# Moving the late rows' normalization from the first two feed-forward groups to the third to sixth, and giving the last output-projection blocks all PSUM banks

## The chip, the cores and the metric

The kernel runs on one core of a Trainium2 chip. The metric is the device time of one execution in microseconds; before the change its median over three runs is 2681.76 us (2677.7 to 2685.48).

The core's engines have instruction queues of their own and run them in order: PE (matmuls, with its weight loads shown apart as PEld), DVE (vector), ACT (scalar and activation), POOL (general elementwise) and SP, which here only issues DMA transfers. Semaphores tie the queues together.

## The reference

One layer of a transformer-like block over 2048 rows of width 1024, in float32: a normed input projection, two kinds of attention, an output projection onto the residual, and a gated feed-forward network of width 2816.

```python
u = rms_norm(h, norm1_w[l])
proj = jnp.einsum('bsd,de->bse', u, w_in[l])
...
mix = jnp.concatenate([y_diff.reshape(b, s, DIFF_HEADS * DIFF_V_DIM),
                       y_sb.reshape(b, s, SB_HEADS * SB_DIM)], axis=-1)
h = h + jnp.einsum('bse,ed->bsd', mix, w_out[l])

u2 = rms_norm(h, norm2_w[l])
gate = jnp.einsum('bsd,df->bsf', u2, w_gate[l])
up = jnp.einsum('bsd,df->bsf', u2, w_up[l])
h = h + jnp.einsum('bsf,fd->bsd', jax.nn.silu(gate) * up, w_down[l])
```

Here `y_diff` is a differential attention (two softmax maps per head) and `y_sb` a stick-breaking attention.

## The kernel before

**Number format.** Every float32 operand is scaled and split into two float16 parts, high and low, and a product is three matmuls (high by high, high by low, low by high). Splitting an operand takes a pass for the high part and one on DVE for the low part (`split_weight`, L221 is the low part).

**Stages.** The 2048 rows are 16 blocks of 128. First come projections and attention, then the output projection (`out_proj`, L832 the matmuls, tiles `po`; L835 the evictions from PSUM onto the residual, on DVE), one call of `next(op)` per block. Its result goes to DRAM as `hd`. The blocks 0 to 11 are normed, transposed (`xtr`) and split at once (`post`), and stored as `xcd`, the left operand of the feed-forward network. The blocks 12 to 15, the **late rows**, are only stored in `hd`; they are needed in the second half of the feed-forward work alone.

**Feed-forward.** The rows are taken in two halves of 1024. Each half runs over 11 groups of 256 columns of the 2816 (`steps`, index `i`, 0 to 21). A group has a `gate` and an `up` product, each as seven block products of a Strassen-like scheme (`quad`, 12 matmuls of 512 columns each: tiles `pa`, `pm`, `pd`), with DVE combining and evicting them (L1047, L1052, L1057, L1067, L1071), and every second group has the `down` product of two groups between its gate and its up (groups 2, 4, 6, 8, 10). In the first half the weights are prepared as they go: `load_ffn` fetches a float32 stage (`stages`, two buffers in turn), squares it on ACT (`sq`, L954, L190), sums the columns with PE (`fsc`, L963 or L183), makes a power-of-two scale and splits (L216 to L221), and stores the result in DRAM (`split`), from which the second half reads it.

**The late rows before.** `build_x` is a generator for the two pairs of blocks (`j` = 2, 3). A tick runs it to its next `yield`: load two row blocks (`bx<-hd`), norm them (L226 on ACT, L229 on DVE), transpose on PE (L1213) and copy back on ACT, then form and split the seven blocks that the scheme needs (`x_ops`) and store them to `xcd`. One tick comes ahead of the first down weight, the others at fourteen places of the groups 0 and 1 (`late_at`). It takes the four `hs` buffers (which `down` uses for the residual rows from group 2 on) and one of the two `wd` buffers. The stage of the second up weight is issued behind the late rows' first two loads (`rows`).

**What sets the order.** The Tile layer schedules the program: it takes the instructions with their dependencies and orders each engine's queue by its own timeline. `high_priority` (PRI) and `issue_after` bend it. So a small edit moves instructions on all engines. PSUM has eight banks: in the feed-forward part `pst` hands them out in turn, six of pool `ps2` and two of pool `psj`; the output projection uses the two of `psj`. `hs`, `act` (the activations, two buffers) and `cg`, `cu` are SBUF tiles with a fixed number of buffers.

Of the kernel before, what the change touches and what calls it, by code (L numbers as in the profile page):

```python
# [11 lines left out]
F32 = mybir.dt.float32  # L12
F16 = mybir.dt.float16
# [3 lines left out]
ALU = mybir.AluOpType  # L17
# [42 lines left out]
def block(tc, a, out):  # L60
# [3 lines left out]
    with top:  # L64
# [192 lines left out]
        with ExitStack() as ph1:  # L257
# [557 lines left out]
            def out_proj():  # L815
                for t in range(NT):
                    mt = pp.tile([P, 2 * D], F16, tag="xt", bufs=3, name=nm("mt"))[:].rearrange("p (k n) -> p k n", k=KT)
                    with tc.high_priority(PRI["wm"]) if PRI["wm"] else nullcontext():
                        mts.append(SP.dma_start(mt, ms[t]))
                    if t in spare:  # L820
                        xf = spare[t].bitcast(F32)
                    else:
                        xf = pp.tile([P, 4, 4, 2, 64], F16, tag="st", name=nm("xf"))[:].rearrange("p c t s e -> p (c t s e)").bitcast(F32)
                    SP.dma_start(xf, x[t * P : (t + 1) * P, :])
                    for h in range(2):
                        po = psj.tile([P, 512], F32, tag="pj", name=nm("po"))
                        for n in range(2):
                            q = 0
                            sl = slice(256 * n, 256 * n + 256)
                            for kt in range(KT):  # L830
                                for xi, wi in ((0, 0), (0, 1), (1, 0)):
                                    PE.matmul(po[:, sl], lhsT=mt[:, kt, P * xi : P * xi + P], rhs=wos[2 * h + n][wi][:, kt, :], start=q == 0, stop=q == 23)  # L832
                                    q += 1
                            xl = xf[:, 512 * h + 256 * n : 512 * h + 256 * n + 256]
                            DVE.scalar_tensor_tensor(xl, po[:, sl], kos[2 * h + n][:], xl, op0=ALU.mult, op1=ALU.add)  # L835
                    note("D", 1400)
                    SP.dma_start(hd[t], xf)
                    if t >= 12:
                        yield
                        continue  # L840
                    post(t, xf)
                    yield
# [31 lines left out]
        with ExitStack() as ph2:  # L874
# [18 lines left out]
            r_2, p_2, r_24 = rp2  # L893
            scales = {}

            rows = []
            front = [None]

            def behind():
# [5 lines left out]
            def stage(fg, nme):  # L905
                st = stages[:, turn[0]]
                turn[0] ^= 1
                f0 = 256 * fg
                with tc.issue_after(rows[1].ins) if (fg, nme) == (1, "u") else nullcontext():
                    fetch(st, f0, nme)  # L910
                store(0)
                return st

# [161 lines left out]
            def gate(W, X, hooks):  # L1075
# [11 lines left out]
                note("A", 2000)  # L1087
                return sg

            def up(W, X, sg, hooks, final=False):  # L1090
                if final:
                    act = stages[:].rearrange("p b n -> p (b n)").bitcast(F16)[:, :7168].rearrange("p (o s n) -> p o s n", o=7, s=2)
                else:
                    act = fp.tile([P, 7, 2, 512], F16, tag="act", bufs=2, name=nm("act"))

                def put(o, src):
                    ACT.copy(act[:, o, 0], src)  # L1097
                    note("A", 500)
                    tt(act[:, o, 1], src, act[:, o, 0], ALU.subtract, 512, LE)

                def on_up(f, t, c):
                    s = sg[f, t][:]
                    DVE.scalar_tensor_tensor(s, c[:], W["F"][:], s, op0=ALU.mult, op1=ALU.mult)  # L1103
                    if (f, t) != (0, 1):
                        put({(0, 0): 0, (1, 0): 1, (1, 1): 3}[f, t], s)
                        return
                    a11, a12, a21, a22 = (sg[k][:] for k in ((0, 0), (1, 0), (0, 1), (1, 1)))
                    s3 = fp.tile([P, 512], F32, tag="cu", bufs=CU, name=nm("cu"))
                    tt(s3[:], a11, a21, ALU.subtract, 512, SE)
                    tt(a21, a21, a22, ALU.add, 512, SE)  # L1110
                    put(2, a21)
                    tt(a11, a21, a11, ALU.subtract, 512, SE)
                    tt(a12, a12, a11, ALU.subtract, 512, SE)
                    put(6, a12)
                    put(4, a11)
                    put(5, s3[:])

                quad(W["u"], X, "cu", CU, on_up, hooks)
                note("D", 2440)
                return act  # L1120
# [66 lines left out]
                        SP.dma_start(out[t * P : (t + 1) * P, :] if last else hd[t], hs[j][q][:])  # L1187

            def build_x():
                w2f, xa, xb, xt = (hp.tile([P, D], F32, tag="hs", bufs=4, name=nm("bx")) for _ in range(4))  # L1190
                SP.dma_start(w2f[:], a["norm2_w"].partition_broadcast(P))
                DVE.tensor_scalar(w2f[:], w2f[:], r_24[:], None, op0=ALU.mult)
                b16 = fd.tile([P, 7, 2, 512], F16, tag="wd", bufs=2, name=nm("b16"))[:].rearrange("p o s n -> p (o s n)")
                n = [0]

                def bufs():
                    n[0] = (n[0] + 1) % 3
                    return b16[:, 2048 * n[0] : 2048 * n[0] + 2048]

                d2 = lambda z: z[:].rearrange("p (d n) -> p d n", d=2)  # L1200
                for j in (2, 3):
                    for q, z in enumerate((xa, xb)):
                        rows.append(SP.dma_start(z[:], hd[8 + 2 * j + q]))
                    yield
                    for z in (xa, xb):
                        norm_tile(z[:], z[:], w2f[:], xt[:])
                    yield
                    for z in (xa, xb):
                        for h in range(2):
                            tr = pst("xtr")  # L1210
                            with behind():
                                for k in range(4):
                                    PE.transpose(tr[:, P * k : P * k + P], z[:, 512 * h + P * k : 512 * h + P * k + P], id32[:])  # L1213
                            ACT.copy(z[:, 512 * h : 512 * h + 512], tr[:])
                        note("A", 1000)
                    yield
                    yield from x_ops([d2(z) for z in (xa, xb)], d2(xt), 1, j, bufs, "AP", "DP")

            W = {}
            X = [None] * 7  # L1220
# [25 lines left out]
                for _ in range(n):  # L1246
                    next(ticks, None)

            tick(1)
            load_now(0, 0, "d", W)  # L1250

            steps = [(h, f) for h in range(2) for f in range(NFG)]
            units = []
            hs = None
            chains = {}
            late_at = ((5, 9, 10, 11, 12, 13, 14), (3, 7, 8, 9, 10, 11, 12))
            for i, (half, fg) in enumerate(steps):
                if i == NFG:
                    load_x(1, XL)
# [13 lines left out]
                    go(key)  # L1273

                def row(s):
                    if i < 2 and s in late_at[i]:
                        tick(1)

                def in_gate(s):
# [66 lines left out]
```

## Time and profile before

| what | value |
|---|---|
| median of three runs | 2681.76 us (2677.7 to 2685.48) |
| the profiled execution | 2682.59 us, of which the span from the first to the last instruction is 2680.8 |
| mean granted clock of PE | 0.984 of full speed |
| PE busy | 2492.4 us (93%) |
| DVE, POOL, ACT busy | 1932.7 (72%), 1489.1 (56%), 1347.0 us (50%) |
| output projection, from first to last matmul | 1179.9 to 1426.9 us |
| feed-forward, from its first to its last gate or up product | 1427.2 to 2621.4 us |
| packets of the main DMA queue | 69.9% of 16 engines' span |

A row of a timeline gives the start and duration in us, the engine, line and operation, the tiles written and read without their numbers, shapes, how many such instructions follow each other, and in brackets how long the engine was idle before it and what released it. L98 and L89 are helpers that many places use, so there the tile names tell the place. PE's matmuls are pipelined: a row's duration is a little longer than the distance to the next one.

### The profile page before, as it was taken

The numbers are of one execution on the slowest core, as the hardware profiler recorded it, in microseconds if no ns is written. First come the engines' busy times: TensorE is split into PE (matmuls) and PEld (weight loads), VectorE is DVE, ScalarE is ACT, GpSimd is POOL, SyncE is SP. The second block draws the span as 40 slices with busy tenths as digits, with TensorE's granted clock in tenths as the row PEclk, the third lists the DMA queues.
The fourth block names the chain that finished last, engine by engine and source line by source line (L and its number), as shares of the span: only waits on it lengthen the run. The fifth ranks groups of instructions, "written<-read, shape, count | busy, mean of one in ns | idle before, by whom it ended". The sixth has DMA issues, their size and how long they took to land. (4 is left out here: it accounts for less than half of the span.)

```text
span 2680.8 us, 50579 instructions
## 1 busy us (share of the span) xinstructions
PE 2492.4 (93%) x19628; PEld 1498.6 (56%) x19628; DVE 1932.7 (72%) x3711; ACT 1347.0 (50%) x2487; POOL 1489.1 (56%) x1098
## 2 busy tenths in 40 slices
PE   6998989888988989889989899999999999999999
PEld 4655656577776776557775344444444444444444
DVE  6898969898989989877766868777685544444434
ACT  4665656567978878665644535344352112111121
POOL 2578667667767766546764656565564232322323
PEclk9999999999999999999999899999999999999999
DMA  6777697767998979987897574665649743635532
GB/s 222 213 162 181 146 200 168 179 143 184 193 179 179 185 160 209 210 191 217 218 285 282 208 250 178 255 226 202 245 183 346 293 177 143 233 141 186 195 111 95
DMA packets 619585, 534.41 MB, mean 199 GB/s; under 512 B 480640, under 2 KB 548224, under 8 KB 609104
## 3 DMA queue, kind: packets, MB, share of 16 engines
q1 hardware_dynamic: 617520, 529.09, 69.9%
q8 instruction: 154, 2.52, 0.4%
q0 software_dynamic: 512, 1.36, 0.2%
q14 instruction: 87, 0.71, 0.1%
q10 hardware_dynamic: 1312, 0.72, 0.1%
HBM read 261.08 MB, written 147.32 MB: 152 GB/s over the span
## 5 line engine op out<-in xcount | busy, mean ns | idle before, releaser
L98 POOL TENSOR_TENSOR s<-z,s 128x1024 f16<-128x1024 f32 (+7 forms) x288 | 472.0, 1647 | 142.5 <-ACT s L89 109.8
L507 PE MATMUL sc<-kT,qT 128*128 128x512 f16 (+3 forms) x1520 | 382.0, 353 | 53.3 <-DVE z L623 19.3
L622 DVE TENSOR_TENSOR_SCAN z<-z,sc 128x512 f32<-128x512 f32 (+3 forms) x320 | 352.8, 1112 | 58.6 <-ACT sc L620 38.0
L1138 PE MATMUL pd<-wd,act 128*128 128x512 f16 x1764 | 390.9, 379 | 1.2 <-DVE cg L1071 1.2
L326 PE MATMUL pj<-w,xt 128*128 128x384 f16 x1920 | 352.2, 331 | 18.8 <-ACT xt L683 6.9
L1030 PEld LDWEIGHTS <-wg 128*128 128x128 f16 x1848 | 182.0, 99 | 230.2 <-issue 16.4
L518 PE MATMUL yp<-v,aT 128*128 128x64 f16 (+1 forms) x4896 | 269.8, 204 | 41.6 <-DMA aT<-s 40.2
L518 PEld LDWEIGHTS <-aT 128*128 128x128 f16 x4896 | 237.5, 99 | 120.4 <-DMA aT<-s 52.5
L1030 PEld LDWEIGHTS <-wu 128*128 128x128 f16 x1848 | 180.7, 98 | 218.0 <-issue 2.6
L98 POOL TENSOR_TENSOR act<-cg,act 128x512 f16<-128x512 f32 x112 | 148.5, 1337 | 262.9 <-ACT act L1097 150.8
L1138 PEld LDWEIGHTS <-act 128*128 128x128 f16 x1764 | 172.8, 98 | 209.4 <-issue 2.8
L326 PEld LDWEIGHTS <-xt 128*128 128x128 f16 x1920 | 187.3, 99 | 147.5 <-issue 21.4
L89 ACT CAST s<-z 128x128 f16<-128x128 f32 (+7 forms) x215 | 173.1, 809 | 134.1 <-DMA aT<-s 40.5
L98 POOL TENSOR_TENSOR hs<-hs,cu 128x512 f32<-128x512 f32 x99 | 130.9, 1328 | 171.3 <-DVE hs L1144 70.8
L619 ACT ACTIVATE z<-sc,c 128x512 f32<-128x512 f32 (+3 forms) x320 | 210.7, 663 | 25.6 <-PE sc L507 11.7
L1097 ACT CAST act<-cg 128x512 f16<-128x512 f32 x126 | 77.3, 616 | 238.4 <-DVE cg L1103 162.7
L507 PEld LDWEIGHTS <-qT 128*128 128x128 f16 x1520 | 128.4, 99 | 121.0 <-DVE z L623 23.0
L832 PE MATMUL po<-wo,mt 128*128 128x256 f16 x1536 | 180.7, 277 | 13.9 <-DVE xf L835 8.4
L1030 PE MATMUL pm<-X,wu 128*128 128x512 f16 x792 | 180.4, 379 | 1.3 <-DVE wu L221 1.3
L1030 PE MATMUL pm<-X,wg 128*128 128x512 f16 x792 | 181.3, 382 | 0.0
L342 PE MATMUL pj<-xt,w 128*128 128x128 f16 x2304 | 175.0, 220 | 6.7 <-DVE v L364 5.7
L1144 DVE SCALAR_TENSOR_TENSOR hs<-pd,c,hs 128x512 f32<-128x512 f32 x136 | 99.0, 747 | 109.6 <-PE pd L1138 83.1
(266 smaller groups left out, 4737.6 us busy)
## 6 DMA issues: line engine op xcount, KB each, us to landing
xt<-xs SPq DMA_DIRECT2D x112, 512.0 KB, 4.3
hs<-hd SPq DMA_DIRECT2D x68, 512.0 KB, 4.5
hd<-hs SPq DMA_DIRECT2D x56, 512.0 KB, 4.7
split<-wg SPq DMA_DIRECT2D x11, 1792.0 KB, 7.8
split<-wu SPq DMA_DIRECT2D x11, 1792.0 KB, 6.7
split<-wd SPq DMA_DIRECT2D x11, 1792.0 KB, 7.2
wg<-split SPq DMA_DIRECT2D x11, 1792.0 KB, 7.3
wd<-split SPq DMA_DIRECT2D x11, 1792.0 KB, 12.2
```

Source lines behind the costliest of these rows:

```text
L89: ACT.copy(dst, src)
L98: (DVE if e == "D" else POOL).tensor_tensor(dst, a_, b_, op)
L326: PE.matmul(pj[:, :384], lhsT=xv[:, xi, kt, :], rhs=G["w"][:, wi, kt, :], start=n == 0, stop=n == 23)
L342: PE.matmul(o, lhsT=x_ if c == 2 else w_, rhs=w_ if c == 2 else x_, start=n == 0, stop=n == 23)
L507: last = PE.matmul(sc[:, : 128 * w].rearrange("p (t n) -> p t n", n=P), lhsT=G["q"][i // 4][:, a_, i % 4, :], rhs=G["k"][q][:, b_, 0:w, :] ...
L518: PE.matmul(yp[:, y0 : y0 + wd], lhsT=aT[:, a_, :], rhs=v[:, v_ : v_ + wd], start=start and j == 0 and q == 0, stop=stop and j == nb - 1 a ...
L619: ACT.activation(om[:, lo:hi], sc[:, :w], AF.Sigmoid, scale=G["nkz"][:])
L622: DVE.tensor_tensor_scan(ov, ov, sc[:, :w], om[:, hi : hi + 1], op0=ALU.mult, op1=ALU.bypass)
L832: PE.matmul(po[:, sl], lhsT=mt[:, kt, P * xi : P * xi + P], rhs=wos[2 * h + n][wi][:, kt, :], start=q == 0, stop=q == 23)
L1030: front[0] = PE.matmul(ps_[:].rearrange("p (t n) -> p t n", n=P), lhsT=wv[:, wo, wi, 128 * kt : 128 * kt + 128], rhs=X[xo][:, :, xi, kt, : ...
L1138: front[0] = PE.matmul(po[:], lhsT=act[:, ao, xi, 128 * j : 128 * j + 128], rhs=W["d"][:, wo, wi, :], start=start and u == 0 and q == 0, s ...
L1144: DVE.scalar_tensor_tensor(dst, po[:], kd[:], src, op0=ALU.mult, op1=ALU.add)
```

## The change

Two things. The output projection's blocks 12 to 15 take their `po` tile from `pst`, so from all eight PSUM banks in turn. And the late rows are taken at ticks in the groups 2 to 5: in group 2 at three places of the up product (after its second, fourth and sixth block product) and in group 3 at the first five places of the gate for the pair `j` = 2, in groups 4 and 5 likewise for `j` = 3. The four `hs` buffers are taken for each pair and not once, so the norm weights are loaded and scaled twice; the split blocks go through an `act` buffer, which the next `up` then takes over, instead of a `wd` buffer; the tick ahead of the first down weight and the `issue_after` on the second up stage are gone.

```diff
@@ out_proj
-                        po = psj.tile([P, 512], F32, tag="pj", name=nm("po"))
+                        po = pst("po") if t >= 12 else psj.tile([P, 512], F32, tag="pj", name=nm("po"))
@@ stage
-                with tc.issue_after(rows[1].ins) if (fg, nme) == (1, "u") else nullcontext():
-                    fetch(st, f0, nme)
+                fetch(st, f0, nme)
@@ up
+            acts = []
+
+            def new_act():
+                return fp.tile([P, 7, 2, 512], F16, tag="act", bufs=2, name=nm("act"))
...
-                    act = fp.tile([P, 7, 2, 512], F16, tag="act", bufs=2, name=nm("act"))
+                    act = acts.pop() if acts else new_act()
@@ build_x
-                w2f, xa, xb, xt = (hp.tile([P, D], F32, tag="hs", bufs=4, name=nm("bx")) for _ in range(4))
-                SP.dma_start(w2f[:], a["norm2_w"].partition_broadcast(P))
-                DVE.tensor_scalar(w2f[:], w2f[:], r_24[:], None, op0=ALU.mult)
-                b16 = fd.tile([P, 7, 2, 512], F16, tag="wd", bufs=2, name=nm("b16"))[:].rearrange("p o s n -> p (o s n)")
...
-                    return b16[:, 2048 * n[0] : 2048 * n[0] + 2048]
+                    return acts[0][:].rearrange("p o s n -> p (o s n)")[:, 2048 * n[0] : 2048 * n[0] + 2048]
...
                 for j in (2, 3):
+                    w2f, xa, xb, xt = (hp.tile([P, D], F32, tag="hs", bufs=4, name=nm("bx")) for _ in range(4))
                     for q, z in enumerate((xa, xb)):
-                        rows.append(SP.dma_start(z[:], hd[8 + 2 * j + q]))
+                        SP.dma_start(z[:], hd[8 + 2 * j + q])
+                    SP.dma_start(w2f[:], a["norm2_w"].partition_broadcast(P))
                     yield
+                    DVE.tensor_scalar(w2f[:], w2f[:], r_24[:], None, op0=ALU.mult)
...
+                    acts.append(new_act())
                     yield from x_ops([d2(z) for z in (xa, xb)], d2(xt), 1, j, bufs, "AP", "DP")
+                    yield
@@ the loop over groups
-            tick(1)
             load_now(0, 0, "d", W)
...
-            late_at = ((5, 9, 10, 11, 12, 13, 14), (3, 7, 8, 9, 10, 11, 12))
+            late_at = {2: (9, 11, 13), 3: (1, 2, 3, 4, 5), 4: (9, 11, 13), 5: (1, 2, 3, 4, 5)}
...
-                    if i < 2 and s in late_at[i]:
+                    if s in late_at.get(i, ()):
                         tick(1)
```

Line numbers shift a little: L1045, L1050 and L1055 of the changed kernel are the former L1047, L1052 and L1057, L961 is the former L963, L1106 the former L1103, L1147 the former L1144 and L1190 the former L1187 (stores of `hs`), L1131 the former L1128 (loads of `hs`). L1203 loads the late rows in both, L1204 and L1206 load and scale the norm weights (before L1191 and L1192), L1215 are the late rows' transposes (before L1213).

More of the change, by code (lines that the diff above doesn't have):

```diff
@@ L894, in block @@
             scales = {}
-            rows = []
             front = [None]
```

## The prediction

> **What bounds the kernel now.** I began with the page's first part, to see which engine fills the span.
>
> ```profile
> span 2680.8 us, 50579 instructions
> PE 2492.4 (93%) x19628; PEld 1498.6 (56%) x19628; DVE 1932.7 (72%) x3711; ACT 1347.0 (50%) x2487; POOL 1489.1 (56%) x1098
> ```
>
> PE is busy 93%, so a change pays where PE waits. Next the busy times by stretch. The columns are the stretch, its length, then busy us and instruction counts of PE, PEld, DVE, ACT and POOL, the granted clock, DMA share and GB/s.
>
> ```profile
> 1465.00:1502.00 37.00, 30.17 (x146) 14.82 (x145) 31.24 (x45) 19.92 (x29) 22.27 (x16) 0.91 0.52 189
> 1502.00:1550.00 48.00, 40.29 (x180) 18.53 (x179) 40.37 (x51) 28.02 (x33) 31.39 (x20) 0.93 0.62 219
> 1550.00:1620.00 70.00, 70.00 (x333) 32.41 (x332) 49.60 (x77) 24.20 (x30) 39.36 (x29) 1.00 0.65 225
> 1602.00:1622.00 20.00, 20.00 (x98) 9.46 (x97) 18.14 (x27) 11.67 (x14) 14.97 (x9) 1.00 0.45 166
> ```
>
> The feed-forward groups start at 1427. In the first three PE loses time (30.17 of 37, 40.29 of 48) at a lowered clock while DVE is busy 84%; from 1550 PE is full. But DVE is nearly full there too between two groups with no down product in between (18.14 of 20 us from 1602). Then the timeline of PE from 1380 on: start, duration, what, and in brackets the idle time before and its releaser.
>
> ```profile
> 1381.34 1.04 PE L665 MATMUL xtr<-id,z 128*128 128x128 f32 x8
> 1382.21 5.18 PE L832 MATMUL po<-wo,mt 128*128 128x256 f16 x46
> 1388.89 1.03 PE L963 MATMUL fsc<-sq,ones 128*128 128x256 bf16 x8 [1.50 <-ACT sq L954]
> 1394.68 5.71 PE L832 MATMUL po<-wo,mt 128*128 128x256 f16 x48 [1.15 <-DVE wo L835]
> 1403.68 3.91 PE L832 MATMUL po<-wo,mt 128*128 128x256 f16 x22 [3.29 <-DVE wo L835]
> 1443.88 2.76 PE L1030 MATMUL pd<-X,wg 128*128 128x512 f16 x12 [0.96 <-DMA X<-xcd]
> 1466.50 2.75 PE L1030 MATMUL pd<-X,wu 128*128 128x512 f16 x12 [1.36 <-DVE cu L1057]
> 1491.13 4.76 PE L1030 MATMUL pd<-X,wg 128*128 128x512 f16 x12 [5.47 <-DVE cg L1057]
> 1517.50 2.75 PE L1030 MATMUL pd<-X,wu 128*128 128x512 f16 x12 [0.64 <-DVE cu L1057]
> 1533.90 1.87 PE L963 MATMUL fsc<-sq,ones 128*128 128x256 bf16 x8 [5.88 <-ACT sq L954]
> 1535.56 7.34 PE L1030 MATMUL pm<-X,wg 128*128 128x512 f16 x24
> 1547.98 1.46 PE L1138 MATMUL pd<-wd,act 128*128 128x512 f16 x6 [1.19 <-DVE cg L1071]
> ...
> 1773.91 4.13 PE L1030 MATMUL pd<-X,wg 128*128 128x512 f16 x12 [3.30 <-DVE cg L1057]
> ```
>
> In the first three groups the waits are 1.36 + 5.47 + 0.64 + 5.88 + 1.19 = 14.5 us. Matmuls behind a long wait are slow as well: 12 products take 4.76 where the row at 1466.50 has 2.75, 24 take 7.34 for twice 2.59 plus 0.16, fsc 1.87 for 1.03. That is 2.0 + 2.0 + 0.8 = 4.8 us more, together 19.3.
>
> **Part one: the late rows leave groups 0 and 1.** Before, DVE does this for them:
>
> ```profile
> L98 DVE TENSOR_TENSOR b<-bx,b x5: 1046/1692/2609, 1468.3 to 1513.4; 128x1024 f16<-128x1024 f32 x3, 128x512 f16<-128x512 f32 x2
> L229 DVE SCALAR_TENSOR_TENSOR bx<-bx,xrs,bx x4: 1906/2160/2284, 1448.8 to 1491.0; 128x1024 f32<-128x1024 f32 x4
> L98 DVE TENSOR_TENSOR bx<-bx x2: 675/676/677, 1466.4 to 1506.6; 128x512 f32<-128x512 f32 x2
> L1192 DVE TENSOR_SCALAR bx<-bx,c x1: 752/752/752, 1445.3 to 1445.3; 128x1024 f32<-128x1024 f32 x1
> L98 DVE TENSOR_TENSOR bx<-bx,bx x1: 1739/1739/1739, 1464.1 to 1464.1; 128x512 f32<-128x512 f32 x1
> ```
>
> By medians that is 5 x 1.69 + 4 x 2.16 + 2 x 0.68 + 0.75 + 1.74 = 20.9 us of DVE between 1445 and 1515, more than the 14.5 us of waits, and it stands in DVE's queue ahead of the operations that PE waits for. Without it the splits and evictions behind which PE stood at the 5.47 and 5.88 waits end earlier by most of that, and both waits go. Late next is L1057 of up 0, the 1.36 wait: it follows the product just ahead on PE and has only part of its cause in late rows. I keep it and 0.6 for chance, 2 us. Term one: -19.3 + 2 = -17.3 (bounds -18 and -9: only half of the waits are the rows').
>
> **Part two: the last four row blocks.** With eight banks the waits of 1.15 and 3.29 for evictions (DVE wo L835) go, with 1.4 us of slow matmuls (22 in 3.91; the 48 at 1394.68 took 5.71, so 22 take about 2.5), and the 0.96 for X is covered since PE comes later. But the order on PE changes too. xtr are transposes of block 11, fsc the column sums of the first gate weight. Before, and then now:
>
> ```order
> L665 MATMUL xtr_21782<-id_63,z_21650 128x128 x4
> L665 MATMUL xtr_21788<-id_63,z_21650 128x128 x4
> L832 LDWEIGHTS mt_21895
> L832 MATMUL po_21898<-wo_17783,mt_21895 128x256
> ...
> L963 LDWEIGHTS ones
> L963 MATMUL fsc_21856<-sq_21853,ones 128x256
> ```
>
> ```order
> L665 MATMUL xtr_21782<-id_63,z_21650 128x128 x4
> L665 MATMUL xtr_21788<-id_63,z_21650 128x128 x4
> L961 LDWEIGHTS ones
> L961 MATMUL fsc_21856<-sq_21853,ones 128x256
> L961 LDWEIGHTS ones
> L961 MATMUL fsc_21856<-sq_21853,ones 128x256
> ```
>
> The 46 po matmuls between them have moved behind fsc, and 17 more from ahead of xtr (42 stand there where 59 did, counted in the order). But fsc needs the squares (ACT, L954) of a stage that a DMA brings, and these released it at 1388.9, whatever PE does. xtr comes 17 x 0.11 = 1.9 us earlier, less 0.8 because both halves of one bank now follow each other, and ends near 1381.3; so PE waits 7.5 us there, where it waited 1.50. Sum: removed 1.50 + 1.15 + 3.29 + 1.4 + 0.96 = 8.3; added 7.5 + 0.8 and about 2.4 of slow matmuls (2.0 to 2.8 behind the 5.47 and 5.88 waits) = 10.7. Term two: +2.4 (bounds -3 if the stage lands early, +5).
>
> **Part three: the late rows in groups 2 to 5.** The 32 transposes cost PE the same 3.5 us as before. What is new is where loads and DVE work stand. SP's queue after the down product of group 2, now:
>
> ```order
> L1190 DMA hd<-hs_23249 128x1024
> L1203 DMA bx_23488<-hd 128x1024
> L1190 DMA hd<-hs_23321 128x1024
> L1190 DMA hd<-hs_23320 128x1024
> L1204 DMA bx_23486<-in_norm_w_dram 128x1024
> L1131 DMA hs_24016<-hd 128x1024
> L923 DMA stages<-in_w_gate_dram 128x8x256
> ```
>
> The norm weights (bx_23486) take a buffer whose last store must land first; behind them SP holds the next hs load and gate stage. On DVE, before and now, from the up product of group 2:
>
> ```order
> L1047 TENSOR_TENSOR cu_23575<-pm_23579,cu_23575 128x512
> L1052 TENSOR_TENSOR cu_23614<-pm_23601,cu_23575 128x512
> L1057 TENSOR_TENSOR cu_23637<-pd_23624,cu_23614 128x512
> L184 TENSOR_REDUCE m_23644<-fsc_23643 128x1
> L1103 SCALAR_TENSOR_TENSOR cg_23222<-cu_23637,c_23006,cg_23222 128x512
> ```
>
> ```order
> L1045 TENSOR_TENSOR cu_23460<-pm_23464,cu_23460 128x512
> L155 TENSOR_SCALAR xrs_23548<-xss_23546 128x1
> L1206 TENSOR_SCALAR bx_23486<-bx_23486,c_17372 128x1024
> L1050 TENSOR_TENSOR cu_23506<-pm_23493,cu_23460 128x512
> L155 TENSOR_SCALAR xrs_23554<-xss_23552 128x1
> L229 SCALAR_TENSOR_TENSOR bx_23487<-bx_23487,xrs_23548,bx_23486 128x1024
> L229 SCALAR_TENSOR_TENSOR bx_23488<-bx_23488,xrs_23554,bx_23486 128x1024
> L1055 TENSOR_TENSOR cu_23529<-pd_23516,cu_23506 128x512
> ```
>
> L1206 waits for that load, and the up product's evictions (L1050, L1055), then the down weight's splits, queue behind it; PE waits for the two L229 (its transposes now stand before the last product of up) and for L1055. When does the load land? The trace of before has the same stores, with the next loads behind them (SP's queue), the lands of norm weights (DMA issues; KB, us to landing), and DVE and PE around:
>
> ```profile
> 1590.50 0.86 SPq L1187 DMA_DIRECT2D hd<-hs  x2
> 1595.72 1.54 SPq L1128 DMA_DIRECT2D hs<-hd  x2
> ...
> bias<-in_norm_w_dram SPq DMA_DIRECT2D x1, 512.0 KB, 4.7
> bx<-in_norm_w_dram SPq DMA_DIRECT2D x1, 512.0 KB, 10.0
> ...
> 1594.53 0.69 DVE L1057 TENSOR_TENSOR cu<-pd,cu 128x512 f32<-128x512 f32 x1 [1.96 <-PE pd L1030]
> 1615.48 1.35 DVE L221 SCALAR_TENSOR_TENSOR wu<-stages,c,wu 128x1024 f16<-128x1024 f32 x1 [1.22 <-ACT wu L216]
> 1616.76 0.68 DVE L1057 TENSOR_TENSOR cg<-pd,cg 128x512 f32<-128x512 f32 x1
> ...
> 1599.67 2.75 PE L1030 MATMUL pd<-X,wu 128*128 128x512 f16 x12
> 1619.11 2.75 PE L1030 MATMUL pd<-X,wg 128*128 128x512 f16 x12
> ```
>
> In before's clock, the load is issued at 1595.7 and lands at 1600.4 by the 4.7 row, at 1605.7 by the 10.0 row (taken while DMA was busy with X; 4.7 is nearer). From there DVE owes L1050 (0.69), the row work of one pair (0.75 + 2 x 2.16 + 0.68 + 1.74 + 2 x 1.69 = 10.9) and what it did in 1594.5 to 1617.4 (22.9, less 1.2 idle, some 0.3 of small gaps and the 1.35 split, which the order puts later: 20.1). That ends at 1632.1 and frees the last product of gate 3, which PE reached at 1619.11, now 1.7 later for 16 transposes: 11.2 us lost. The lower end is the transposes' own wait: the L229 by their shortest, 1600.4 + 0.75 + 0.69 + 3.8 = 1605.6 against 1599.67, less 0.9 for transposes in between: 5.0.
>
> The second pair stands likewise after group 4's down; there xtr stand behind the last product of up.
>
> ```profile
> 1704.48 0.40 SPq L1187 DMA_DIRECT2D hd<-hs  x1
> 1705.78 6.97 SPq L1128 DMA_DIRECT2D hs<-hd  x2
> ...
> 1710.00 0.75 DVE L1103 SCALAR_TENSOR_TENSOR cg<-pa,c,cg 128x512 f32<-128x512 f32 x1 [0.21 <-PE pa L1030]
> 1727.77 4.15 DVE L221 SCALAR_TENSOR_TENSOR wu<-stages,c,wu 128x1024 f16<-128x1024 f32 x2 [0.62 <-ACT wu L216]
> 1732.51 0.68 DVE L1057 TENSOR_TENSOR cg<-pd,cg 128x512 f32<-128x512 f32 x1
> 1734.17 2.75 PE L1030 MATMUL pd<-X,wg 128*128 128x512 f16 x12
> 1735.06 1.91 ACT L954 ACTIVATE sq<-stages 128x2048 bf16<-128x2048 f32 x1 [0.48 <-DVE wu L221]
> ```
>
> The junk buffer of the squares is free when the store of 1704.48 has landed, about 1712.4; squares of 1.3 us let DVE go on at 1713.7. It owes 23.2 us (1710.00 to 1733.2), less 4.2 + 0.7 of later splits and 0.6 idle, plus 10.9: 1742.3, against PE's 1734.17 + 1.7: 6.4 us (lower end 3). Behind each late gate product the next stage's squares (1.91) follow the splits that were moved back, with two products of PE as cover: 1.5 us each, at most 3.5. Term three: +11.2 + 6.4 + 3 = +20.6 (bounds +8 and +32, the upper with the 10.0 landing in both, 3.5 twice and a slow start of 1.4, as at 1773.91, each).
>
> On the clock the row says that 3.30 us of waiting already slows 12 products by 1.4. [...]
>
> **Sum.** -17.3 + 2.4 + 20.6 = +5.7. The profiled execution took 2682.59 us (span 2680.8 and 1.8 around it), 0.8 over the median 2681.76; so 2688.3 in that frame and 2687.5 as a median. 0.3% (8 us) is about what can be told from no change.
>
> **Rivals.** (a) Faster: the DVE queue catches up, and only the transposes' waits remain (+8), the stage lands early (0), 18 is gained: -10, 2672. For it: DVE idles 30% over 1550 to 1620. Against: not from 1602. (b) Slower: the norm weights land by the 10.0 row and the squares follow late; cost 32 against 17.3, and +5 in part two: +20, 2702. It decides from a cost of 23 up. (c) Slower: half of the first groups' waits are the weight chain's own (the weight splits run on DVE there with or without late rows, and 9 of the 18 us stay): -9 + 2.4 + 20.6 = +14, 2696. For it: fsc at 5.88 waited for ACT, not DVE; against: 20.9 us of DVE. That the change does nothing is excluded by the orders above.
>
> **Chances.** Forecast (within 0.3%) 0.42; (a) 0.23, so faster 0.23; (b) 0.22 and (c) 0.13, so slower 0.35. Cases of both signs hold much, so the forecast's own range is 2680 to 2694; the 8-in-10 range reaches to (a) and (b): 2669 to 2703.
>
> **What would show it.** Right: no wait over 2 us in groups 0 to 2; the first down product near 1532; one wait of 6 to 8 us for fsc about 1381; waits for DVE at the transposes and at L1055 in gates 3 and 5, 15 to 20 us together. Wrong: waits of 5 us left before 1530 (c), or transposes that start at once (a).

## The result: 0.7% slower, at the upper end of the range

The changed kernel takes 2702.52 us (median of six runs, 2694.84 to 2705.39), the kernel before 2681.39 beside it (six runs, 2677.7 to 2688.14). The ratio is 1.0072, with a 95% interval of 1.0057 to 1.0086: 19 us lost, 15 to 23. The page's first part hardly shows it: all busy times are those of before within 6 us, on a longer span.

```profile
PE 2498.3 (92%) x19628; PEld 1500.5 (56%) x19628; DVE 1935.1 (72%) x3711; ACT 1345.7 (50%) x2488; POOL 1485.3 (55%) x1098
```

The busy times by stretch show where it lies. The first two rows are groups 0 to 2, where before PE did 30.17 of 37 us; the last two are gate 3 and gate 5, where before PE was full but for one wait of 0.66 us.

```profile
1465.00:1502.00 37.00, 37.00 (x182) 17.50 (x180) 28.91 (x43) 19.44 (x23) 20.89 (x15) 1.00 0.41 157
1502.00:1539.00 37.00, 33.43 (x162) 15.80 (x161) 30.12 (x42) 21.04 (x24) 24.34 (x17) 1.00 0.55 203
...
1588.00:1621.00 33.00, 22.66 (x114) 11.20 (x113) 30.76 (x44) 16.56 (x24) 19.86 (x13) 0.95 0.53 183
1720.00:1753.00 33.00, 23.11 (x116) 11.31 (x114) 31.57 (x37) 18.74 (x27) 23.55 (x15) 0.96 0.53 185
```

PE lost 10 us in each of the last two, with DVE busy 93 to 96% of them. PE's timeline gives the waits one by one (tail of the output projection, groups 0 to 2, groups 2 and 3, groups 4 and 5):

```profile
1392.27 1.86 PE L961 MATMUL fsc<-sq,ones 128*128 128x256 bf16 x8 [6.42 <-ACT sq L952]
...
1455.57 2.75 PE L1028 MATMUL pd<-X,wg 128*128 128x512 f16 x12 [2.00 <-DMA X<-xcd]
...
1531.33 1.45 PE L1141 MATMUL pd<-wd,act 128*128 128x512 f16 x6 [1.96 <-ACT cg L1081]
1536.98 1.46 PE L1141 MATMUL pd<-wd,act 128*128 128x512 f16 x6 [1.61 <-DVE cg L1069]
...
1591.20 1.09 PE L1215 MATMUL xtr<-id,bx 128*128 128x128 f32 x8 [2.36 <-DVE bx L229]
1593.03 1.06 PE L1215 MATMUL xtr<-id,bx 128*128 128x128 f32 x8 [0.73 <-DVE bx L229]
...
1620.51 4.62 PE L1028 MATMUL pd<-X,wg 128*128 128x512 f16 x12 [6.42 <-DVE c L205]
1630.75 1.51 PE L961 MATMUL fsc<-sq,ones 128*128 128x256 bf16 x8 [3.03 <-ACT sq L952]
1632.06 6.59 PE L1028 MATMUL pm<-X,wu 128*128 128x512 f16 x24
...
1724.79 1.06 PE L1215 MATMUL xtr<-id,bx 128*128 128x128 f32 x8 [1.08 <-DVE bx L229]
1726.44 1.09 PE L1215 MATMUL xtr<-id,bx 128*128 128x128 f32 x8 [0.58 <-DVE bx L229]
1734.06 2.75 PE L1028 MATMUL pm<-X,wg 128*128 128x512 f16 x12 [1.35 <-DVE cu L1069]
...
1752.33 5.26 PE L1028 MATMUL pd<-X,wg 128*128 128x512 f16 x12 [6.88 <-DVE cg L1055]
```

In the tail stands one long wait, 6.42 for fsc. Of groups 0 to 2 only the 2.00 for X (the left operand, from DRAM) is left up to 1531. The late rows bring 2.36 + 0.73 + 6.42 + 3.03 us of waits in groups 2 and 3 (0.84 more for an fsc between) and 1.08 + 0.58 + 1.35 + 6.88 in groups 4 and 5, each long one with slow matmuls behind it (12 products in 4.62 and 5.26 for 2.75). The row of 6.42 names L205, a step of 0.14 us right behind L1055 on DVE; L1055 itself ends at 1620.45, as PE starts.

Executions differ by up to 13 us in the attention stage, which no kernel here changes: its last transposes of y (L489) start between 1365.95 and 1379.22 us in the profiled runs. So the table counts from there: to **B**, the start of the long run of down products of group 2 (1539.25 in the changed kernel); to **C**, the first product of gate 4; and to the end of the span. All are starts in PE's timelines (for before 1374.68, 1550.24, 1640.49, and the span of 2680.8). These three columns and their sum come from one profiled execution each. The last column is the ratio of the timed medians, from 6 to 12 runs of each kernel beside the kernel before.

| kernel | to B | B to C | C to end | sum, against before | ratio to before (95%) |
|---|---|---|---|---|---|
| before | 175.6 | 90.3 | 1040.3 | 1306.1 | |
| changed | 160.0 | 109.8 | 1053.8 | +17.6 | 1.0072 (1.0057 to 1.0086) |
| banks only | 179.5 | 90.3 | 1040.7 | +4.3 | 1.0017 (1.0004 to 1.0029) |
| banks for 14 and 15 | 173.9 | 90.3 | 1040.4 | -1.7 | 0.9995 (0.9983 to 1.0007) |
| rows only | 153.1 | 109.4 | 1054.1 | +10.6 | 1.0036 (1.0022 to 1.0050) |
| no late rows | 158.2 | 90.3 | 1039.8 | -17.9 | 0.9926 (0.9911 to 0.9940) |
| changed, no norm | 160.1 | 97.7 | 1049.6 | +1.2 | 1.0001 (0.9989 to 1.0013) |
| rows only, norm on ACT | 154.1 | 103.7 | 1056.1 | +7.8 | 1.0019 (1.0007 to 1.0031) |
| before, norm on ACT | 178.4 | 90.6 | 1038.9 | +1.7 | 1.0003 (0.9992 to 1.0015) |
| each pair two groups earlier | 163.7 | 108.4 | 1040.2 | +6.2 | 1.0017 (1.0006 to 1.0027) |
| rows only, all on DVE | 152.4 | 106.5 | 1055.5 | +8.3 | 1.0051 (1.0038 to 1.0064) |
| before, all on DVE | 175.2 | 91.5 | 1040.2 | +0.9 | 1.0001 (0.9990 to 1.0013) |
| rows only, behind the eviction | 152.3 | 109.5 | 1055.9 | +11.5 | 1.0055 (1.0039 to 1.0072) |
| before, behind the eviction | 169.0 | 90.3 | 1040.2 | -6.7 | 0.9980 (0.9969 to 0.9991) |

### The profile page after: what moved, and what is told of

It reads as the page before. It is cut to its first block, busy times and chain, and to the rows that moved or that the text cites. A ratio compares the mean times of both kernels' runs of the same rounds, so it can differ in the third digit from the quotient of the medians.

```text
span 2702.9 us, 50594 instructions
## 1 busy us (share of the span) xinstructions
PE 2498.3 (92%) x19628; PEld 1500.5 (56%) x19628; DVE 1935.1 (72%) x3711; ACT 1345.7 (50%) x2488; POOL 1485.3 (55%) x1098
## 3 DMA queue, kind: packets, MB, share of 16 engines
q0 software_dynamic: 512, 1.36, 0.2%
## 4 chain that ended last, share of the span: by engine, by line
PE 38%; DVE 6%; DMA 2%; issue 2%; POOL 1%; ACT 1%; SPq 0%; DVEq 0%; ACTq 0%; POOLq 0%
PE pd L1141 12%; PE pm L1028 10%; PE pa L1028 7%; PE pd L1028 7%; DMA hd<-hs 1%; DVE wd L221 1%; PE po L832 1%; DVE cg L98 1%; DVE wu L221 1%; PE fsc L961 1%; POOL hs L98 1%; DVE cg L1106 0%; DMA X<-xcd 0%; DMA hs<-hd 0%; DVE act L98 0%
## 5 line engine op out<-in xcount | busy, mean ns | idle before, releaser
L98 POOL TENSOR_TENSOR s<-z,s 128x1024 f16<-128x1024 f32 (+7 forms) x288 | 471.3, 1645 | 146.5 <-ACT s L89 116.0
L98 POOL TENSOR_TENSOR act<-cg,act 128x512 f16<-128x512 f32 x114 | 152.4, 1347 | 249.4 <-ACT act L1100 137.3
L98 POOL TENSOR_TENSOR hs<-hs,cu 128x512 f32<-128x512 f32 x99 | 130.7, 1328 | 171.5 <-DVE hs L1147 71.5
L1147 DVE SCALAR_TENSOR_TENSOR hs<-pd,c,hs 128x512 f32<-128x512 f32 x136 | 99.1, 747 | 109.9 <-PE pd L1141 83.3
```

The source lines that it names most:

```text
L98: (DVE if e == "D" else POOL).tensor_tensor(dst, a_, b_, op)
L1147: DVE.scalar_tensor_tensor(dst, po[:], kd[:], src, op0=ALU.mult, op1=ALU.add)
```

## The experiments

### The two parts apart

**Banks only**, the kernel before with one line of the change:

```diff
-po = psj.tile([P, 512], F32, tag="pj", name=nm("po"))
+po = pst("po") if t >= 12 else psj.tile([P, 512], F32, tag="pj", name=nm("po"))
```

> The kernel before with only part two: blocks 12 to 15 of the output projection take po from all eight banks, late rows as before. The prediction's term was +2.4 us, so 2683.8. The trace of the changed kernel had 6.42 us for fsc and lost 4.6 over the tail: by that 2686. Rival: the 4.5 us that the changed kernel was already behind at the last instruction both kernels share ahead of the tail belong to this part too (a layout effect): then 2690. Rival on the other side: the stage lands early here, and the two eviction waits go for nothing: 2678.

Measured: 2685.95 us against 2681.36, +4.6. PE's timeline has the wait that the order foretold, and a longer one for X:

```profile
1379.51 1.87 PE L963 MATMUL fsc<-sq,ones 128*128 128x256 bf16 x8 [6.93 <-ACT sq L954]
...
1440.56 2.76 PE L1030 MATMUL pd<-X,wg 128*128 128x512 f16 x12 [2.35 <-DMA X<-xcd]
```

6.93 where before has 1.50, and 2.35 where it has 0.96. The part costs 4 us, and the 4.5 us by which the changed kernel was late ahead of the tail do not belong to it: here the same transposes start 8.7 us earlier than before. **Banks for 14 and 15** (`t >= 14`) leaves fsc behind its po matmuls:

> The kernel before with the eight banks for blocks 14 and 15 only. The column sums of the first gate weight then keep their place on PE (the 46 po matmuls stay ahead of them). Theory (part two loses because fsc has moved ahead of those matmuls and waits 6.4 to 6.9 us for squares that come no earlier): the wait of about 7 us stays away and the eviction waits of 1.15 and 3.29 go in part: 3 us less than before, 2678. Rival (any use of the eight banks in this stretch only passes the wait on, to the next fsc or to X): 2683 to 2686.

Measured: 2681.07 against 2682.23, no difference that can be told. The long wait is gone, as the theory says, but so is the gain: the eviction waits stay.

```profile
1385.99 1.03 PE L963 MATMUL fsc<-sq,ones 128*128 128x256 bf16 x8 [0.64 <-ACT sq L954]
...
1400.80 2.56 PE L832 MATMUL po<-wo,mt 128*128 128x256 f16 x22 [3.29 <-DVE wo L835]
```

**Rows only**, the changed kernel with `po` from `psj` for all blocks:

> The changed kernel with the two-bank po for all blocks: the late rows' move alone. If the two parts add up, as the sum of the prediction assumed, it is the changed kernel less part two: 2702.5 - 4.6 = 2698 (2693 if part two has the 9 us). The prediction's terms one and three gave -17.3 + 20.6 = +3.3, 2684.7. Rival: the parts interact (the loss in the tail moves X or the down weight so that the first groups start elsewhere): anything else, above all a time at or over the changed kernel's.

Measured: 2691.69, +10.3. With +4.6 for the banks this makes 14.9 against the 19 to 21 of both; from the common point it is 4.3 + 10.6 = 14.9 against 17.6. The intervals allow a sum; the cause of the 2.7 us between is open. The traces put them ahead of B: this kernel has no wait for X at all there, the changed one 2.00.

### What the late rows cost at each place

**No late rows**, with `po` from `psj` (it leaves out the late rows' normalization; their places in the operand are filled by storing blocks 8 to 11 twice, so the last 512 rows of the result are not the reference's):

```diff
-late_at = {2: (9, 11, 13), 3: (1, 2, 3, 4, 5), 4: (9, 11, 13), 5: (1, 2, 3, 4, 5)}
+late_at = {}
```

> Leaves out the late rows' normalization altogether (no ticks); their places in the split operand are filled by a second store of blocks 8 to 11, so the output of the last 512 rows is not the reference's. Two-bank po. It prices the late rows at each place: before minus this is what they cost in groups 0 and 1, the rows-only kernel minus this is what they cost in groups 2 to 5. Theory (the late rows' DVE work makes the waits of groups 0 to 2): 17.3 and 3.5 of transposes less than before, 2660.6; in the first three groups no wait over 2 us. Rival (the weight chain's own waits): 9 + 3.5 less, 2669, and waits of about 2.5 to 3 us stay at the two places that had 5.5 and 5.9.

Measured: 2663.16, 18.2 us under before, 28.5 under rows only. In groups 0 to 2 one wait for X is left, and the two at the down products that the changed kernel has too (1.95 and 1.62 here):

```profile
1449.81 4.44 PE L1030 MATMUL pd<-X,wg 128*128 128x512 f16 x12 [3.10 <-DMA X<-xcd]
...
1527.25 1.45 PE L1143 MATMUL pd<-wd,act 128*128 128x512 f16 x6 [1.95 <-ACT cg L1083]
```

So every wait of 5 us in groups 0 to 2 was the late rows', and rival (c) falls. This kernel is 5.1 us behind rows only at B, all of it from the tail and the wait for X: from the first fsc behind that wait both take 81.1 us to B. **Each pair two groups earlier** (`late_at = {0: (9, 11, 13), 1: (1, ..., 5), 2: (9, 11, 13), 3: (1, ..., 5)}`):

> The rows-only kernel with each pair two groups earlier: pair 2 at the places of groups 0 and 1, pair 3 at those of groups 2 and 3. The kernel without late rows is at 2663. If each pair has a price of its own at its place: 18 / 2 = 9 for the pair in groups 0 and 1, and 19 for the one in groups 2 and 3 (the difference of the two kernels over that stretch): 2691, no gain over the rows-only kernel. Rival (one pair fits into DVE's idle share in groups 0 and 1 and costs little more than its transposes, 2): 2684. Rival (a price per pair that is the same everywhere, 14): 2691 as well, but then with waits of 5 us or more at L1055 of gate 1.

Measured: 2688.15, +5.9. To B it is 10.6 us over rows only, of which 2.4 lie ahead of the first fsc behind X and 8.2 in the groups 0 to 2; B to C is 18.1 over before, as with a pair there in rows only (19.2). A pair has its own price at its place: some 8 in groups 0 and 1, 18 to 19 in groups 2 and 3, 14 in groups 4 and 5 (C to end, 13.8), its 1.75 us of transposes with it.

### What makes the price: amount of DVE work, or something else

**No norm**, the changed kernel without the two L229, L1206, the squares and the root:

> The changed kernel, leaving out the late rows' multiplication by the norm weights and the reciprocal root (squares on ACT, two small steps, L1206 and the two L229 on DVE); loads, buffers, transposes, copies, splits and stores stay. Theory (what DVE owes between the rows' landing and gate 3's and 5's L1055 sets the waits, one to one): some 5 us less per pair (0.75 + 2 x 1.3 to 2.2), and the transposes' own waits (2.36 + 0.73, 1.08 + 0.58) go: the L1055 waits of 6.42 and 6.88 fall to about 2, slow matmuls with them: 12 us less, 2690. Rival (the place itself, that is loads, hs and act buffers handed over, sets the end): the waits move elsewhere and the time stays within 3 us of the changed kernel, 2700.

Measured: 2681.92, 20.6 under the changed kernel (16.3 from the common point), more than expected, and not as expected: gate 3's wait falls only to 3.58, gate 5's hardly.

```profile
1602.64 4.44 PE L1028 MATMUL pd<-X,wg 128*128 128x512 f16 x12 [3.58 <-DVE cg L1055]
...
1725.81 4.70 PE L1028 MATMUL pd<-X,wg 128*128 128x512 f16 x12 [6.60 <-DVE cg L1055]
```

What went besides were PE's waits at the transposes and for the squares. This left open whether DVE's work or the long path through the norm was paid for. **Norm on ACT** computes all of it, without L229 on DVE and with a load of 4 KB for 512, at the late place and at the early one (`norm_act` is `norm_tile` with `ACT.mul(z, z, rs[:])` in place of DVE's multiplication):

```diff
-norm_tile(z[:], z[:], w2f[:], xt[:])
+norm_act(z[:], xt[:])
...
-ACT.copy(z[:, 512 * h : 512 * h + 512], tr[:])
+for k in range(4):
+    ACT.mul(z[:, 512 * h + P * k : 512 * h + P * k + P], tr[:, P * k : P * k + P], w2f[:, 4 * h + k : 4 * h + k + 1])
```

> The rows-only kernel (2691.7 us; late rows in groups 2 to 5, two-bank po) with the late rows' norm taken off DVE: ACT multiplies a row by its reciprocal root, and applies the norm weights, one per partition, while it copies the transposed rows from PSUM (16 pieces of 128 columns per pair instead of 4 of 512). The 512 KB load of norm weights becomes one of 4 KB. All is computed. DVE theory: 5 us less DVE work per pair ahead of the two L1055, as in the run without the norm, which was 16 us shorter behind the common point; ACT's longer path to the transposes gives some of it back: 2679 (2675 to 2684). Rival (hand-over of buffers and the rows' own latency set the transposes and all behind them): 2688 to 2692, with waits for ACT at the transposes where there were waits for DVE.

> The kernel before (2681.4 us; late rows in groups 0 and 1) with the same move of the norm to ACT. Late rows cost 18 us there and give DVE 20.9 us, of which the norm is 0.75 + 4 x 2.16 = 9.4. If the cost goes with DVE's work: 18 x 9.4 / 20.9 = 8 less, 2673, and the waits of 5.47 and 5.88 us shrink to 2 to 3. Rival: these two waits come from the rows' splits (L98, up to 2.6 us each), which stand last ahead of the eviction and the squares: 2679 to 2682.

Measured: 2687.83 late (3.9 under rows only, 12.7 expected) and 2684.59 early (2682.23 before: no change, 8 expected). Late, the waits stay as long or go to the next weight:

```profile
1600.88 5.13 PE L1028 MATMUL pd<-X,wg 128*128 128x512 f16 x12 [7.02 <-DVE cg L1055]
...
1704.86 3.54 PE L1223 MATMUL xtr<-id,bx 128*128 128x128 f32 x16 [4.07 <-ACT bx L1197]
1729.44 4.45 PE L1028 MATMUL pm<-X,wu 128*128 128x512 f16 x10 [4.19 <-DVE wu L221]
```

and early they are longer than before (5.47 and 5.88):

```profile
1490.20 5.15 PE L1030 MATMUL pd<-X,wg 128*128 128x512 f16 x12 [6.30 <-DVE cg L1057]
...
1534.04 1.87 PE L963 MATMUL fsc<-sq,ones 128*128 128x256 bf16 x8 [6.56 <-ACT sq L954]
```

The late kernel did gain with the first pair: B to C is 5.7 us shorter than in rows only (103.7 for 109.4), and L1055 of gate 3 starts 2.4 us sooner behind B, though PE, which comes there sooner as well, waits as long. With the second pair it lost 2.0 (C to end), with 4.07 of waiting for ACT at the transposes and a wait of 4.04 in gate 6 with a slow start, where rows only waits 3.31 with none. Moreover DVE's queue was held up as before, with the small load as with the large one:

```profile
1570.31 0.23 DVE L1214 TENSOR_SCALAR bx<-bx,c 128x8 f32<-128x8 f32 x1 [8.06 <-DMA bx<-in_norm_w_dram]
```

That is 47.9 us behind B, where L1206 of rows only starts at 48.9; in the kernel without norm, whose queue has no such step, the up product's L1050 runs 41.6 behind B instead of 50.0 in the changed kernel. So this run took off DVE's work but not its waiting for the rows and the load.

The sum of DVE's work, the currency of the prediction, is not enough for a second reason. The rows of the changed kernel in gate 3 show it: first DVE, then GpSimd (POOL) beside it.

```profile
1588.54 0.75 DVE L1206 TENSOR_SCALAR bx<-bx,c 128x1024 f32<-128x1024 f32 x1 [1.13 <-DMA bx<-in_norm_w_dram]
...
1604.31 2.02 DVE L98 TENSOR_TENSOR bx<-bx,bx 128x512 f32<-128x512 f32 x1
...
1608.60 0.68 DVE L98 TENSOR_TENSOR bx<-bx 128x512 f32<-128x512 f32 x1
...
1619.77 0.68 DVE L1055 TENSOR_TENSOR cg<-pd,cg 128x512 f32<-128x512 f32 x1
```
```profile
1603.20 2.58 POOL L98 TENSOR_TENSOR act<-bx,act 128x1024 f16<-128x1024 f32 x1
...
1609.50 1.51 POOL L98 TENSOR_TENSOR bx<-bx,bx 128x512 f32<-128x512 f32 x1 [2.04 <-DVE bx L98]
```

The same 128x512 operation on two SBUF tiles takes 0.68 us at 1608.60, where POOL is idle (from 1607.5 to 1609.5), and 2.02 at 1604.31 beside POOL. L1055 at 1619.77 and L1045 at 1613.69, which read PSUM, take 0.68 each beside POOL's operations. (The first row is the norm weights' scaling, which waited for their load.) Counted over all DVE operations with two SBUF inputs, each less the shortest of its form (0.69 and 1.21 for L98, 0.74 and 1.28 for L221), DVE is lengthened by 7.0 us between 1588.5 and 1620.5 and by 9.0 between 1720.8 and 1752.3. With the norm on ACT it was 8.2 for the first pair (1570.0 to 1600.8), so 1.2 of the 3.3 us of DVE work taken off there (0.75 + 2 x 1.28) came back. **All on DVE** takes the late rows' four POOL operations per pair over to DVE:

```diff
-(DVE if e == "D" else POOL).tensor_tensor(dst, a_, b_, op)
+(DVE if e == "D" or rows_on[0] else POOL).tensor_tensor(dst, a_, b_, op)
```

> The rows-only kernel (2691.7 us) with all differences and low parts of the late rows on DVE; before, GpSimd did four of the ten per pair (6.7 us of it for pair 2). All is computed. In the traces DVE operations with two SBUF inputs took 0.69 us (128x512) with GpSimd idle and up to 2.0 beside a GpSimd operation; those with a PSUM input never changed. Theory one (the sum of DVE work alone sets L1055 of gates 3 and 5): 3 x 0.69 + 1.2 = 3.3 us more DVE per pair, 2698. Theory two (DVE and GpSimd slow each other, so GpSimd's share comes back on DVE): the stretch of pair 2 had 6.0 us of such lengthening, of which GpSimd's late-row operations are 6.7 of 17 us there, so 2.4 come back per pair and the net is +0.9 each: 2693. If most of the lengthening came from these four: 2686.

> The kernel before (2682 us; late rows in groups 0 and 1) with the same move of the late rows' GpSimd operations to DVE. The run with the norm off DVE at this place changed neither the time nor the waits of 6.30 and 6.56 us, so DVE's total is not what counts here. Theory one (work of DVE in the queue): more of it, 2687. Theory two (GpSimd's late-row operations lengthen DVE's and come ahead of the weight differences that the splits and squares wait for): the two waits shrink by 2 us each, 2677 to 2680.

Measured: 2694.02 late (ratio 1.0051 against 1.0036 for rows only) and 2682.48 early (2680.35 before). The timing of the late one does not decide between the theories: its interval overlaps that of rows only and takes in theory one as well. The trace, of one execution, speaks against theory one: from the common point it is 2.3 us shorter than rows only, with 3.3 us more of DVE operations per pair. The groups of DVE operations up to gate 3's eviction, of the changed kernel and then of this one, where L98 is L100 (busy us, mean ns), show what pays for them:

```profile
L98 DVE TENSOR_TENSOR cg<-cg,cg 128x512 f32<-128x512 f32 x3 | 4.2, 1405 | 0.0
L98 DVE TENSOR_TENSOR act<-bx,act 128x1024 f16<-128x1024 f32 x2 | 3.9, 1934 | 0.0
```
```profile
L100 DVE TENSOR_TENSOR act<-bx,act 128x1024 f16<-128x1024 f32 x3 | 3.6, 1212 | 0.0
...
L100 DVE TENSOR_TENSOR cg<-cg,cg 128x512 f32<-128x512 f32 x3 | 2.1, 687 | 0.0
```

Three operations take less time than two did; the lengthening falls from 7.0 to 2.9 us in gate 3 and from 9.0 to 6.1 in gate 5. So what such operations took on DVE depended here on what POOL did beside them, and in these runs neither moving the late rows' work between the two nor part of it to ACT made the price small. In the early kernel one wait fell by about the 2 us that theory two promised (5.47 to 3.71), the one for the squares did not (5.88 to 6.07), and a new one came at the down products, so that the time stayed:

```profile
1491.55 4.44 PE L1032 MATMUL pd<-X,wg 128*128 128x512 f16 x12 [3.71 <-DVE cg L1059]
...
1544.36 2.72 PE L1140 MATMUL pd<-wd,act 128*128 128x512 f16 x6 [3.14 <-ACT cg L1085]
```

### The order in DVE's queue

The last two put the late rows' DVE work behind the eviction `c22` for which PE waits (`issue_after` is the planner's edge): at the late place the splits and differences, with ticks (4, 5, 6, 7, 7), at the early one all of it, with the second norm two places later (5 for 3). The early edit:

```diff
-DVE.tensor_tensor(c22[:], pd[:], u3[:], ALU.add)
+dfront[0] = DVE.tensor_tensor(c22[:], pd[:], u3[:], ALU.add).ins
...
-next(ticks, None)
+with tc.issue_after(dfront[0]) if dfront[0] is not None else nullcontext():
+    next(ticks, None)
```

> The rows-only kernel (2691.7 us) with the late rows' splits and differences put behind the eviction c22 (L1055 there, L1056 here) of the gates 3 and 5 in DVE's queue: their ticks move to the fourth to seventh place of the gate, and an edge to the eviction's instruction keeps the planner from pulling them ahead. In the order the four or five DVE operations that stood ahead of the eviction of gate 3 are gone from there; three follow it. Theory (PE waits because the eviction stands behind late-row work in DVE's queue): the waits of 6.41 and 6.88 us fall to 1 to 3, their slow matmuls (2.1 and 2.5) go, and some of it comes back as waits for the up weight, whose splits now stand behind the late rows: 8 to 12 us less, 2682. Rival (DVE simply owes this work by the next weight, wherever it stands): the waits move to the up products, 2689 to 2692.

> The kernel before (2681 us; late rows in groups 0 and 1) with the same edge: every DVE operation of the late rows stands behind the latest eviction c22 (L1057 there, L1058 here), and the second pair's norm comes two places later in gate 1. In the order both L229 (1.9 to 2.3 us each) move from ahead of that eviction in gate 1 to behind it, and two L98 behind the evictions of up 1. Theory: the wait of 5.47 us falls by 2 to 4 with part of its 2.0 us of slow matmuls, those of 1.36 and 0.64 go, the 5.88 for the squares stays: 4 to 6 us less, 2676, the first version below the kernel before. Rival (the splits of the up weight, which stay ahead of the eviction, end last): the wait stays over 4.5, 2680 to 2682.

Late, 2695.56 (ratio 1.0055): no gain; the rival's account, though 4 us above its time. The wait at the eviction falls to 3.14 and 4.91 come for the next squares, behind the up weight's splits; in group 5 all of it moves to the up weight:

```profile
1600.50 4.44 PE L1029 MATMUL pd<-X,wg 128*128 128x512 f16 x12 [3.14 <-DVE cg L1056]
...
1614.12 1.87 PE L962 MATMUL fsc<-sq,ones 128*128 128x256 bf16 x8 [4.91 <-ACT sq L953]
...
1735.47 4.45 PE L1029 MATMUL pm<-X,wu 128*128 128x512 f16 x10 [4.15 <-DVE wu L221]
```

Early, 2675.53, ratio 0.9980 (0.9969 to 0.9991): the only version that computes everything and is faster than the kernel before by more than the noise, by 5.6 us. On DVE, before and then here, the first L229 has moved from ahead of the splits and the eviction of gate 1 to behind them:

```profile
1484.25 2.17 DVE L229 SCALAR_TENSOR_TENSOR bx<-bx,xrs,bx 128x1024 f32<-128x1024 f32 x1
1486.34 3.48 DVE L221 SCALAR_TENSOR_TENSOR wu<-stages,c,wu 128x1024 f16<-128x1024 f32 x2
...
1490.40 0.68 DVE L1057 TENSOR_TENSOR cg<-pd,cg 128x512 f32<-128x512 f32 x1
```
```profile
1477.74 3.56 DVE L221 SCALAR_TENSOR_TENSOR wu<-stages,c,wu 128x1024 f16<-128x1024 f32 x2 [0.60 <-ACT wu L216]
...
1481.88 0.68 DVE L1058 TENSOR_TENSOR cg<-pd,cg 128x512 f32<-128x512 f32 x1
...
1484.84 2.48 DVE L229 SCALAR_TENSOR_TENSOR bx<-bx,xrs,bx 128x1024 f32<-128x1024 f32 x2 [0.45 <-POOL xrs L156]
```
```profile
1482.62 4.26 PE L1031 MATMUL pd<-X,wg 128*128 128x512 f16 x12 [4.80 <-DVE xrs L155]
...
1523.97 1.87 PE L964 MATMUL fsc<-sq,ones 128*128 128x256 bf16 x8 [4.29 <-ACT sq L955]
```

The waits of 1.36 and 0.64 are gone, as expected; those of 5.47 and 5.88 are 4.80 and 4.29, with 4.26 for 4.76 behind the first; one of 1.3 for ACT is new. The first fell less than the 2 to 4 us expected, since the splits stay ahead of the eviction (the rival's reason), the second more. Some 2 of the 6.7 us from the common point lie in the tail, where fewer po matmuls were slow in this execution. In groups 0 and 1 the order decided part of the price; in gates 3 and 5 the work that was moved is owed by the next weight wherever it stands. How much of the early gain is the edge's and how much the later second norm's, no run separates.

## Why the range held and its middle was too low

The likeliest case, no change at 2687.5, did not come; the time is that of rival (b), at the edge of the range.

**Term one** (-17.3, with 3.5 us of transposes counted as going elsewhere: -20.8 to B) held. Rows only is 22.4 us shorter to B, of which 2.3 are a tail without the 0.96 for X and with 22 po matmuls in 2.56 for 3.91: 20.1. The kernel without late rows gives the same 20.1 (17.4 to B, and a tail that is 2.7 longer than before's). No wait over 2 us is left there, as named, if only just (2.00 for X). That the first down product starts at 1531.33, near the 1532 named, is partly luck: the run was 4.5 us late at the common point.

**Term two** (+2.4, bounds -3 and +5) measured +4.0 to +4.6 alone. The wait of 7.5 for fsc came as 6.42 to 6.93, the 0.8 for two halves of one bank in a row as a wait of 0.63 for an eviction (1382.20 in the changed kernel, released by L835); a longer wait for X (2.0 to 2.35, where 0.96 was to go) was not in the term.

**Term three** (+20.6) was mis-sized: B to the end grew by 33 us in rows only and in the changed kernel, less 3.5 of transposes 29.5, near its upper bound of 32. Its mechanism is in the trace step by step. The norm weights' load let DVE go on at 1588.5, 49.3 behind B, where 1600.4 with B at 1550.24 meant 50.2: rival (b)'s landing by the 10.0 row is false. For the first pair 11.2 us of waits were named up to gate 3's L1055 and 2.36 + 0.73 + 0.84 + 6.42 = 10.4 came. What failed is, first, that slow matmuls behind the new waits were priced in terms one and two and left out of the third but for its upper bound: 4.62 + 1.51 + 6.59 us for what takes 2.75 + 1.03 + 5.34, so 3.6, and 2.5 behind the 6.88. Second, the second pair's waits: 6.4 named and 9.9 come (1.08 + 0.58 + 1.35 + 6.88). From gate 4 on the changed kernel runs 8.6 us behind the clock of before (1649.06 for 1640.49). By that clock L1055 was named to end at 1750.9, and it ended at 1752.3: DVE went on 1.5 sooner than named (1720.8 for 1722.3), but its work took 31.5 for 28.6. Its durations were taken from before and hold some 8.0 us of lengthening (5.9 in 1710.0 to 1733.2, less 1.7 in the splits taken off, and 3.8 in the medians of the row work); it was 9.0, and L1206 took 1.61 for 0.75 besides. The other 2.0 are PE's order, which the term took as it was. Before, nine matmuls of up 5 stood ahead of gate 5's last product, the last seven behind a short wait:

```profile
1732.65 1.69 PE L1030 MATMUL pm<-X,wu 128*128 128x512 f16 x7 [0.66 <-DVE wu L221]
```

In the changed kernel they come behind it, and PE stands idle where they had filled the time. Together 3.6 + 2.5 + 3.5 = 9.6, less the 0.8 by which the first pair's waits were over-priced: 8.8 of the 8.9 that were missing. This sum leaves out the small gaps at each wait and, the other way, gate 6, whose 12 products behind a wait of 3.3 ran in 2.75 here and in 4.13 before. The squares had 3 us and took 3.03.

So rival (b)'s time came by another way: the loads were on time, and too low were the price of a wait for PE (6.1 us of slow matmuls) and that of the second pair. Rival (a) fell at gate 3's 6.42, rival (c) with the kernel without late rows.

## What to carry to other kernels

A wait that was moved here brought its slow restart with it: in the stretches looked at, waits of over 4 us cost 1.3 to 3.0 us more behind them, and some of 2 to 3.6 us up to 1.7. Count that on the side that is added as on the side that is removed. Work for DVE was not a number of its own here: a 128x512 operation on two SBUF inputs took 0.68 us with POOL idle and up to 2.02 beside POOL's (up to 2.61 with the norm on ACT), so in a stretch where both are busy, price both engines together, and prefer to move work to where both idle. Before work is moved to other groups, look whether its order in the queue, behind the one eviction that PE waits for, buys the same: here that gave 5.6 us where the move cost 10.

## What was not expected of the hardware

**Equal waits, unequal restarts.** A wait of 3.3 us for the same eviction, in gate 6, left the 12 products behind it at 2.75 us in some runs and cost 1.3 to 1.7 us in others; a wait of 2.09 for another eviction cost 1.5. Rows of the rows-only kernel, of banks for 14 and 15, and of before with the norm on ACT:

```profile
1783.47 2.75 PE L1028 MATMUL pd<-X,wg 128*128 128x512 f16 x12 [3.31 <-DVE cg L1055]
```
```profile
1770.19 4.23 PE L1030 MATMUL pd<-X,wg 128*128 128x512 f16 x12 [3.30 <-DVE cg L1057]
```
```profile
1463.27 4.24 PE L1030 MATMUL pd<-X,wu 128*128 128x512 f16 x12 [2.09 <-DVE cu L1057]
```

The changed kernel has this wait with 2.75 us behind it as well (3.31 at 1796.54), before has it with 4.13 (3.30 at 1773.91). The granted clock behind the first of these two is 1.00 (1796.5 to 1799.3); behind the second it is 0.78 from 1774 to 1776 and 0.50 from 1776 to 1778. So the length of a wait alone did not tell here what the matmuls behind it took; what else decides it no run shows.

**DVE beside GpSimd.** 0.68 us became up to 2.02 in the gates 3 and 5 of the changed kernel for two SBUF inputs (up to 2.61 with the norm on ACT) and stayed between 0.67 and 0.69 for a PSUM input (the 220 operations of L1045, L1050, L1055, L1065 and L1069). The lengthening of 1.34 us at 1604.31 is near the 1.47 us that POOL's operation of 1603.20 still had to run. One operation with a single SBUF tensor showed it too: L1206, 0.75 at 1588.54, took 1.61 at 1721.66 beside POOL's operation of 1721.56; what lengthened it no run shows.
